# Seven block products for three pairs of k-tiles in the feed-forward layers, and for the query and output projections of attention

## The chip, the core and the metric

The kernel runs on one core of a Trainium2 chip. TensorE (PE) multiplies, VectorE (DVE) and ScalarE (ACT) do elementwise work, and SyncE (SP) issues the transfers that bring weights from memory. The metric is the time of one execution in microseconds (us), the median of several runs.

## What is computed

The reference runs one two-layer network and then another on 256 tokens of width 2048, all in float32. The parts that the change touches belong to the first network:

```python
x = x + s5_mixer(h, ...)                    # layer 0; ends in a gated projection with w_glu (GLU)
k, v = shared_kv(x, kv_norm, w_kv, k_norm)  # layer 1: rmsnorm(x, kv_norm) @ w_kv
x = x + dilated_attention(h, k, v, q_norm, w_q, w_o)   # h = rmsnorm(x, mix_norm); 3 query groups
x = x + swiglu_ffn(rmsnorm(x, ffn_norm), w_gate_up, w_down)   # after both layers
```

The second network (two mixers with projections `w_in_2` and `w_out_2`) follows; the change does not touch it.

## The kernel before

**A float32 product in three.** Every float32 operand is split in two: `hi`, its value rounded to the type fp32r of the matrix engine, and `lo`, the remainder. A product of a token tile and a weight tile is then three matmuls, hi*hi, hi*lo and lo*hi. ACT makes `whi` (a cast) and DVE makes `wlo` (the raw weight less `whi`), two tiles of 512 columns at a time (128x1024). `whi` and `wlo` have four buffers each (`WB`), and the raw ring `wraw` has two.

**Plain products.** `gemm` goes over 16 k-tiles of 128 rows and makes 512 output columns for both halves of the tokens: 16 x 2 x 3 = 96 matmuls of 512 columns.

**Paired products.** `gemm_pair` makes two blocks of 512 columns at once (a gate block and its up block; two neighbouring blocks of the down projection). The tokens' two halves and the two column blocks form a 2x2 block product, and for some of the k-tiles it is made with seven products in place of eight (Strassen's scheme in the form with four token sums S1 to S4, which `forms` has prepared, and four weight sums t1 to t4, which DVE makes each time, line 155). In what follows this is the *S phase*. It takes two pairs of k-tiles: 7 products x 2 pairs x 3 = 42 matmuls, with the weights b11, t3, t2, t4, b21, t1, b22 in this order. The other k-tiles go directly, two k-tiles to a unit of 24 matmuls (the *D phase*): 144 matmuls where there are 16 k-tiles. At the end four additions (line 230) combine the banks; for a gate-up pair ACT then makes `silu` and DVE the product `midt` (line 346, "gated"), and in the next pair's D phase the `turn` transposes `midt` on PE (8 transposes, line 269) and splits it (`act_hi` on ACT, `act_lo` on DVE). For the first chunk of each group of four `turn` also makes the token sums `mf` of the down projection (lines 115 to 124), in tiles of a pool of their own (`wt`).

**Order.** Each engine runs its instructions in the order of its own list. PE, DVE, ACT and SP have lists that a scheduler made when the kernel was built; an instruction at the head of a list that waits holds all behind it. SP issues transfers in its list's order, and each waits until the tile it overwrites has been read.

**Counts.** There are 3 pairs in the GLU stage, 10 gate-up and 6 down pairs in each feed-forward layer (`ffn` 0 and 1), and attention in four groups of heads (`hc`), each with five plain products of 16 k-tiles, then the output projection as plain products of 4 k-tiles.

Of the kernel before, what the change touches and what calls it, by code (L numbers as in the profile page):

```python
# [19 lines left out]
KT = D // 128  # L20
# [8 lines left out]
def load_unit(k, W, r0, nk, c0, cw):  # L29

    nc = k.nc
    raw = k.wraw.tile([128, 4, 512], F32, name="wraw")
    nc.sync.dma_start(
        raw[:, :nk, :cw],
        W[r0:r0 + nk * 128, c0:c0 + cw].rearrange("(k p) c -> p k c", p=128),
    )
    parts = []
    for a in range(0, nk, 2):
        n = min(2, nk - a)
        hi = k.whi.tile([128, 2, 512], F32R, name="whi")  # L40
# [14 lines left out]
def gemm(k, xT, groups, W, c0, cw, late=0):  # L55
# [18 lines left out]
    for i, g in enumerate(groups):  # L74
        with behind(k, k.lo_at), behind(k, k.sp_at):
            parts = load_unit(k, W, g[0][1], len(g), c0, cw)
# [16 lines left out]
class Strassen:  # L93
# [12 lines left out]
    def block(self):  # L106
        return self.pool.tile([128, 2, 512], F32, name="wt", bufs=3)

    def forms(self, xT, kt0, name):

        k, nc = self.k, self.k.nc
        xh, xl = (x[:, kt0:kt0 + 4, :] for x in xT)
        hi, lo = (self.pool.tile([128, 4, 2, 128], F32R, name=f"{name}_{n}") for n in ("hi", "lo"))
        x = self.block().rearrange("p q (i t) -> p (q i) t", i=2)
        nc.vector.tensor_tensor(x, xh.bitcast(F32), xl.bitcast(F32), ALU.add)
        x = x.rearrange("p (q i) t -> p q i t", i=2)
        a11, a12, a21, a22 = (x[:, :, i, t * 128:(t + 1) * 128] for t in range(2) for i in range(2))
        sm = self.block().rearrange("p a (b t) -> p (a b) t", t=128).rearrange("p (f q) t -> p f q t", q=2)
        nc.vector.tensor_tensor(sm[:, 0], a21, a22, ALU.add)
        nc.vector.tensor_tensor(sm[:, 2], a11, a21, ALU.subtract)  # L120
        nc.vector.tensor_tensor(sm[:, 1], sm[:, 0], a11, ALU.subtract)
        nc.vector.tensor_tensor(sm[:, 3], a12, sm[:, 1], ALU.subtract)
        nc.scalar.copy(hi, sm)
        nc.vector.tensor_tensor(lo, sm, hi.bitcast(F32), ALU.subtract)
        return kt0, hi, lo

    def split(self, src):

        k, nc = self.k, self.k.nc
        hi = k.whi.tile([128, 2, 512], F32R, name="whi")  # L130
        lo = k.wlo.tile([128, 2, 512], F32R, name="wlo")
# [4 lines left out]
    def gemm_pair(self, xT, forms, kts, W, row0, cols, apart=False):  # L136
# [5 lines left out]
        kt0, sh, sl = forms  # L142
        xh, xl = xT
        raw = self.pool.tile([128, 2, 2, 2, 512], F32, name="wraw4")
        for n, c0 in enumerate(cols):
            for q in range(2):
                r0 = row0 + (kt0 + 2 * q) * 128
                nc.sync.dma_start(raw[:, q, :, n, :], W[r0:r0 + 256, c0:c0 + 512].rearrange("(i p) c -> p i c", p=128))
        b11, b12, b21, b22 = (raw[:, :, i, n, :] for i in range(2) for n in range(2))
# [3 lines left out]
        def total(a, b):  # L153
            t = self.block()
            nc.vector.tensor_tensor(t, a, b, ALU.subtract)  # L155
            return t

        def product(o, form, w, start):
            wh, wl = self.split(w)
            for q in range(2):  # L160
                if form in blocks:
                    i, t = blocks[form]
                    a, b = (x[:, kt0 + 2 * q + i, t * 128:(t + 1) * 128] for x in xT)
                else:
                    a, b = (x[:, int(form[1]) - 1, q, :] for x in (sh, sl))
                nc.tensor.matmul(o, a, wh[:, q], start=start and q == 0, stop=False, skip_group_check=True)  # L166
                nc.tensor.matmul(o, a, wl[:, q], start=False, stop=False, skip_group_check=True)  # L167
                k.mm = nc.tensor.matmul(o, b, wh[:, q], start=False, stop=q == 1, skip_group_check=True).ins  # L168

        def kept(o, name):  # L170
            e = self.pool.tile([128, 512], F32, name=name)
# [17 lines left out]
        direct = [kt for kt in kts if not kt0 <= kt < kt0 + 4]  # L189
# [3 lines left out]
        def jobs():  # L193
            nonlocal called
            called += 1
            for job, rate in list(k.jobs):
                for _ in range(8 * rate * called // calls - 8 * rate * (called - 1) // calls):
# [5 lines left out]
        for g in range(last + 1):  # L203
# [7 lines left out]
            parts = [self.split(raw[:, j]) for j in range(2)]  # L211
# [111 lines left out]
def ffn(ctx, k, layer):  # L323
    nc, I = k.nc, k.I
    work = ctx.enter_context(k.tc.tile_pool(name="ffnw", bufs=2))
# [7 lines left out]
    mforms = []  # L333
    for s0 in range(0, nch, 4):
        n = min(4, nch - s0)
        mid = act_pair(k, 0)
        for c in range(s0, s0 + n):
            m = work.tile([128, 2, 512], F32, name="midt")

            def silu(t, g):  # L340
                sil = work.tile([128, 512], F32, name="sil")
# [6 lines left out]
            if c == 0:  # L348
                pg = gemm(k, xT, kgroups(), wgu, 0, 512)
                sils = [silu(t, pg[t]) for t in range(2)]  # L350
                forms = st.forms(xT, 12, "xf")
# [8 lines left out]
            def turn(m=m, c=c, s0=s0):  # L360
# [3 lines left out]
                if c == s0:  # L364
                    mforms.append(st.forms(mid, 0, "mf"))

            meanwhile(k, turn)
        for nn in range(0, 4, 2):
            pd, rest = st.gemm_pair(
                mid, mforms[-1], range(4 * n), wd, s0 * 512, (nn * 512, nn * 512 + 512), apart=True  # L370
# [543 lines left out]
def glu(ctx, k, gT):  # L914
# [21 lines left out]
    forms = st.forms(gT, 12, "xf")  # L936
# [50 lines left out]
def attention(ctx, k):  # L987
# [12 lines left out]
    xq, xkv = act_pair(k, 0), act_pair(k, 1)  # L1000
# [3 lines left out]
    split_transposed(k, xs, xkv, list(range(KT)), gkv)  # L1004
    split_transposed(k, xs, xq, list(range(KT)), gq)
# [3 lines left out]
    def project(hc):  # L1009
# [3 lines left out]
        def turned(name, pool, x, W, col, gcol):  # L1013
            kk = head_norm(k, p2, gemm(k, x, kgroups(), W, col, 512), rstd)
# [6 lines left out]
        turned("kT", p2, xkv, wkv, c0, kg)  # L1021
        vv = out["vv"] = p2.tile([128, 2, 512], F32, name="vv")
        ps = gemm(k, xkv, kgroups(), wkv, 2048 + c0, 512)
        for t in range(2):
            nc.scalar.activation(vv[:, t, :], ps[t], AF.Copy, scale=rstd[:, t:t + 1])
        for g in range(3):
            turned(f"qT{g}", p2 if g == 0 else p1, xq, wq, g * 2048 + c0, qg[:, g:g + 1])
        return out

    def heads(hc, pj):  # L1030
        yield
        kT, qT, vv = pj["kT"], [pj[f"qT{g}"] for g in range(3)], pj["vv"]
# [629 lines left out]
```

## Time and profile before

| | |
|---|---|
| median of 3 runs | 3208.32 us (3207.38 to 3209.45) |
| profiled execution: own time | 3209.36 us |
| its span | 3207.6 us |
| busy: PE, DVE, ACT | 98%, 71%, 54% of the span |
| mean granted clock of PE | 0.996 of full |

The stages follow each other along the span: the state-space mixer to about 161 us, GLU to 335, `ffn` 0 to 1045, attention to about 1640 (its transposes begin at 1043), `ffn` 1 to 2357, the second network to the end. A busy share is a mean over all of them. A matmul of 512 columns is listed with a duration of 390 ns, but matmuls are pipelined, so their cost is the distance from one start to the next.

### The profile page before, as it was taken

The numbers are of one execution on the slowest core, as the hardware profiler recorded it, in microseconds if no ns is written. First come the engines' busy times: TensorE is split into PE (matmuls) and PEld (weight loads), VectorE is DVE, ScalarE is ACT, GpSimd is POOL, SyncE is SP. The second block draws the span as 40 slices with busy tenths as digits, with TensorE's granted clock in tenths as the row PEclk, the third lists the DMA queues.
The fourth block names the chain that finished last, engine by engine and source line by source line (L and its number), as shares of the span: only waits on it lengthen the run. The fifth ranks groups of instructions, "written<-read, shape, count | busy, mean of one in ns | idle before, by whom it ended". The sixth has DMA issues, their size and how long they took to land.

```text
span 3207.6 us, 43406 instructions
## 1 busy us (share of the span) xinstructions
PE 3137.0 (98%) x16872; PEld 2671.6 (83%) x16883; DVE 2277.0 (71%) x3421; ACT 1728.8 (54%) x2335; POOL 13.8 (0%) x23
## 2 busy tenths in 40 slices
PE   4999999999999999999999999999999999999998
PEld 4788888888888888888888888888889898899887
DVE  8967777777777665756768777777858566575564
ACT  6355655455555655545455555545556455564463
POOL 1000000000000000000000000000000000000000
PEclk9999999999999999999999999999999999999999
DMA  3265655665555555454565565566555557456554
GB/s 55 85 216 171 210 182 186 209 210 194 200 197 178 171 168 177 163 189 158 168 204 186 195 201 184 182 207 210 184 162 166 184 152 221 158 165 202 155 182 170
DMA packets 343215, 573.96 MB, mean 179 GB/s; under 512 B 55073, under 2 KB 106785, under 8 KB 342177
## 3 DMA queue, kind: packets, MB, share of 16 engines
q1 hardware_dynamic: 309344, 561.91, 53.5%
q10 hardware_dynamic: 33664, 9.28, 1.4%
q8 instruction: 132, 2.16, 0.3%
q14 instruction: 75, 0.61, 0.1%
HBM read 568.51 MB, written 2.62 MB: 178 GB/s over the span
## 4 chain that ended last, share of the span: by engine, by line
PE 91%; DVE 3%; ACT 3%; DMA 2%; issue 0%; SPq 0%; ACTq 0%; another core or an unknown queue 0%; DVEq 0%
PE psg L71 14%; PE psg L69 14%; PE psg L70 14%; PE psg L220 11%; PE psg L221 11%; PE psg L222 11%; PE psg L166 4%; PE psg L167 3%; PE psg L168 3%; PE psm L269 1%; PE psg L399 1%; DMA wraw<-in_w_in 1%; DVE S L399 1%; PE psm L1044 1%; DVE sc L399 1%; ACT VW L399 1%
## 5 line engine op out<-in xcount | busy, mean ns | idle before, releaser
L43 DVE TENSOR_TENSOR wlo<-wraw,whi 128x1024 fp32r<-128x1024 f32 (+1 forms) x560 | 628.1, 1131 | 467.9 <-ACT whi L42 466.6
L42 ACT CAST whi<-wraw 128x1024 fp32r<-128x1024 f32 (+1 forms) x560 | 540.8, 978 | 640.1 <-PE psg L71 377.1
L133 DVE TENSOR_TENSOR wlo<-wraw,whi 128x1024 fp32r<-128x1024 f32 x509 | 608.4, 1222 | 279.5 <-ACT whi L132 277.1
L69 PE MATMUL psg<-whi,act_hi 128*128 128x512 f32 (+1 forms) x2144 | 802.8, 374 | 0.9 <-DVE act_lo L399 0.7
L71 PE MATMUL psg<-whi,act_lo 128*128 128x512 f32 (+1 forms) x2144 | 796.4, 372 | 4.1 <-DVE act_lo L279 4.1
L70 PE MATMUL psg<-wlo,act_hi 128*128 128x512 f32 (+1 forms) x2144 | 796.2, 371 | 0.8 <-DVE wlo L43 0.8
L132 ACT CAST whi<-wraw 128x1024 fp32r<-128x1024 f32 x509 | 522.8, 1055 | 488.7 <-DMA wraw<-in_w_gate_up 168.5
L220 PE MATMUL psg<-whi,act_hi 128*128 128x512 f32 x1616 | 630.8, 390 | 0.8 <-ACT whi L132 0.8
L221 PE MATMUL psg<-wlo,act_hi 128*128 128x512 f32 x1616 | 628.9, 389 | 0.8 <-DVE wlo L133 0.8
L222 PE MATMUL psg<-whi,act_lo 128*128 128x512 f32 x1616 | 628.8, 389 | 0.0
L71 PEld LDWEIGHTS psg<-whi,act_lo 128*128 128x128 f32 x2144 | 403.2, 188 | 59.9 <-DVE act_lo L279 5.0
L69 PEld LDWEIGHTS psg<-whi,act_hi 128*128 128x128 f32 x2144 | 403.6, 188 | 55.6 <-issue 1.3
L70 PEld LDWEIGHTS psg<-wlo,act_hi 128*128 128x128 f32 x2144 | 403.7, 188 | 53.7 <-DVE wlo L43 1.5
L220 PEld LDWEIGHTS psg<-whi,act_hi 128*128 128x128 f32 x1616 | 303.4, 188 | 63.6 <-ACT whi L132 1.2
L221 PEld LDWEIGHTS psg<-wlo,act_hi 128*128 128x128 f32 x1616 | 303.4, 188 | 63.4 <-DVE wlo L133 1.1
L222 PEld LDWEIGHTS psg<-whi,act_lo 128*128 128x128 f32 x1616 | 303.3, 188 | 63.1
L132 ACT CAST whi<-wt 128x1024 fp32r<-128x1024 f32 x140 | 147.7, 1055 | 119.7 <-PE psg L222 101.7
L133 DVE TENSOR_TENSOR wlo<-wt,whi 128x1024 fp32r<-128x1024 f32 x140 | 170.8, 1220 | 50.4 <-ACT whi L132 50.3
L155 DVE TENSOR_TENSOR wt<-wraw 128x1024 f32<-128x1024 f32 x70 | 84.3, 1220 | 8.4 <-DMA wraw<-in_w_down 6.7
L155 DVE TENSOR_TENSOR wt<-wraw,wt 128x1024 f32<-128x1024 f32 x70 | 85.5, 1221 | 1.1
L168 PE MATMUL psg<-whi,act_lo 128*128 128x512 f32 x210 | 82.0, 390 | 0.0
L167 PE MATMUL psg<-wlo,act_hi 128*128 128x512 f32 x210 | 81.9, 390 | 0.0
(359 smaller groups left out, 2931.6 us busy)
## 6 DMA issues: line engine op xcount, KB each, us to landing
wraw<-in_w_gate_up SPq DMA_DIRECT2D x320, 512.0 KB, 4.7
wraw<-in_w_down SPq DMA_DIRECT2D x176, 512.0 KB, 5.1
wraw<-in_w_in SPq DMA_DIRECT2D x96, 768.0 KB, 4.7
wraw<-in_w_q SPq DMA_DIRECT2D x48, 1024.0 KB, 5.1
wraw<-in_w_kv SPq DMA_DIRECT2D x32, 1024.0 KB, 5.5
wraw<-in_w_in SPq DMA_DIRECT2D x32, 1024.0 KB, 5.0
wraw<-in_w_out SPq DMA_DIRECT2D x32, 1024.0 KB, 5.1
wraw<-in_w_glu SPq DMA_DIRECT2D x48, 512.0 KB, 4.7
```

The source lines that it names most:

```text
L42: k.act_at = nc.scalar.copy(hi[:, :n, :cw], raw[:, a:a + n, :cw]).ins
L43: k.dve_at = nc.vector.tensor_tensor(lo[:, :n, :cw], raw[:, a:a + n, :cw], hi[:, :n, :cw].bitcast(F32), ALU.subtract).ins
L69: nc.tensor.matmul(o, a, wh, start=n == 0, stop=False)
L70: nc.tensor.matmul(o, a, wl, start=False, stop=False)
L71: k.mm = nc.tensor.matmul(o, b, wh, start=False, stop=n == total - 1).ins
L132: k.act_at = nc.scalar.copy(hi, src).ins
L133: k.dve_at = nc.vector.tensor_tensor(lo, src, hi.bitcast(F32), ALU.subtract).ins
L167: nc.tensor.matmul(o, a, wl[:, q], start=False, stop=False, skip_group_check=True)
L168: k.mm = nc.tensor.matmul(o, b, wh[:, q], start=False, stop=q == 1, skip_group_check=True).ins
L220: nc.tensor.matmul(o, a, wh[:, n], start=False, stop=False, skip_group_check=True)
L221: nc.tensor.matmul(o, a, wl[:, n], start=False, stop=False, skip_group_check=True)
L222: k.mm = nc.tensor.matmul(o, b, wh[:, n], start=False, stop=g == last and j == 1, skip_group_check=True).ins
```

## The change

The seven-product scheme now takes a list of group sizes. In GLU, in both gate-up projections and in the down projection of `ffn` 0 the sizes are (2, 1), three pairs of k-tiles: 63 matmuls in the S phase and 120 in the D phase, 183 in place of 186. The down projection of `ffn` 1 keeps two pairs, (2,). Each group has a raw tile (`sraw0` of 128x1024 per block, `sraw1` of 128x512), and every split, weight sum and form is made once per group. The weight sums t1 and t3 are computed in place over b11 and b12 (before they had tiles of their own), and t4 over t2; b21's product now stands ahead of t4's. The token sums use a tile of the ring `wraw` in place of the pool's own tiles, and in the `ffn` they are made in the turns of the first two chunks of a group in `ffn` 0, of the first in `ffn` 1.

In attention the tokens are transposed and split once (before: once for k and v, once for q). The norm weights that differ are multiplied into the weight tiles (`split_scaled`, one instruction per 512 columns on ACT and on DVE, where the plain split had one per 1024). Query groups 0 and 1 are one pair with sizes (2,), and so are the blocks of the output projection, which is now made at the end over all 16 k-tiles, two pairs, while the last heads run.

```diff
+def split_scaled(k, hi, lo, src, g):
+    k.act_at = k.nc.scalar.activation(hi, src, AF.Copy, scale=g).ins
+    k.dve_at = k.nc.vector.scalar_tensor_tensor(lo, src, g, hi.bitcast(F32), ALU.mult, ALU.subtract).ins
...
-        return self.pool.tile([128, 2, 512], F32, name="wt", bufs=3)
...
+    def fill(self, forms, xT, groups=None):
+        kt0, sizes, hi, lo = forms
+        for g in range(len(sizes)) if groups is None else groups:
+            m, q0 = sizes[g], sum(sizes[:g])
+            room = k.wraw.tile([128, 4, 512], F32, name="wraw")
...
-        raw = self.pool.tile([128, 2, 2, 2, 512], F32, name="wraw4")
...
+        for g, m in enumerate(sizes):
+            raws.append(self.pool.tile([128, m, 2, 2, 512], F32, name=f"sraw{g}"))
...
+        if gain is not None:
...
+                        nc.scalar.activation(r[:, q, i], r[:, q, i], AF.Copy, scale=gain[:, q0:q0 + 1])
...
         product(c22, "A11", b11, True)
         p1 = kept(c22, "st_p1")
-        product(c21, "S3", total(b22, b12), True)
+        t1 = less(b11, b12, b11)
+        t3 = less(b12, b22, b12)
+        t2 = less([self.pool.tile([128, m, 512], F32, name=f"wt{g}") for g, m in enumerate(sizes)], b22, t1)
+        product(c21, "S3", t3, True)
         p7 = kept(c21, "st_p7")
-        t1 = total(b12, b11)
-        t2 = total(b22, t1)
         product(c22, "S2", t2, False)
         u2 = kept(c22, "st_u2")
-        product(c21, "A22", total(b21, t2), False)
+        t4 = less(t2, b21, t2)
         product(c11, "A12", b21, True)
+        product(c21, "A22", t4, False)
...
-    work = ctx.enter_context(k.tc.tile_pool(name="ffnw", bufs=2))
+    work = ctx.enter_context(k.tc.tile_pool(name="ffnw", bufs=1))
...
+    forms = st.new_forms(KT - 6, "xf")
...
+        mforms = st.new_forms(0, "mf", (2, 1)[:2 - layer])
...
-                if c == s0:
-                    mforms.append(st.forms(mid, 0, "mf"))
+                if c - s0 < len(mforms[1]):
+                    st.fill(mforms, mid, (c - s0,))
...
-    split_transposed(k, xs, xkv, list(range(KT)), gkv)
-    split_transposed(k, xs, xq, list(range(KT)), gq)
+    split_transposed(k, xs, xT, list(range(KT)))
...
-        for g in range(3):
-            turned(f"qT{g}", p2 if g == 0 else p1, xq, wq, g * 2048 + c0, qg[:, g:g + 1])
+        pq = st.gemm_pair(xT, forms, range(KT), wq, 0, (c0, 2048 + c0), gain=gq, keep=places())
+        for g in range(2):
+            turned(f"qT{g}", p1, [pq[t][g] for t in range(2)], qg[:, g:g + 1])
+        turned("qT2", p1, gemm(k, xT, kgroups(), wq, 2 * 2048 + c0, 512, gain=gq), qg[:, 2:3])
...
+    for n in range(0, 4, 2):
+        po, rest = st.gemm_pair(
+            aT, forms, range(KT), wo, 0, (n * 512, n * 512 + 512), apart=True, keep=places()
+        )
```

**DVE around the start of a pair.** These are rows of DVE's list in `ffn` 0 where the third gate-up pair follows the second; `wraw_4716` (later `sraw_4805` and `sraw_4810`) holds the new pair's raw weights, and the lines 230 and 272, 346 and 389 are the last pair's bank additions and its gated products. Before:

```order
L133 TENSOR_TENSOR wlo<-wraw_4716,whi 128x1024
L133 TENSOR_TENSOR wlo<-wt,whi 128x1024
L230 TENSOR_TENSOR psg<-psg,st_u_4424 128x512
L230 TENSOR_TENSOR psg<-psg,st_p_4408 128x512
L155 TENSOR_TENSOR wt<-wraw_4716,wt 128x1024
L346 SCALAR_TENSOR_TENSOR midt<-psg,rstd,sil 128x512
L230 TENSOR_TENSOR psg<-psg,st_p_4394 128x512
L230 TENSOR_TENSOR psg<-psg,st_u_4458 128x512
L133 TENSOR_TENSOR wlo<-wt,whi 128x1024
L346 SCALAR_TENSOR_TENSOR midt<-psg,rstd,sil 128x512
L133 TENSOR_TENSOR wlo<-wt,whi 128x1024
L133 TENSOR_TENSOR wlo<-wraw_4716,whi 128x1024
```

After, the rows from t3's first half on; ahead of them stand `wlo` of b11 in two parts with t1's first half (line 186) between them:

```order
L186 TENSOR_TENSOR sraw_4805<-sraw_4805 128x2x512
L272 TENSOR_TENSOR psg<-psg,st_u_4523 128x512
L272 TENSOR_TENSOR psg<-psg,st_p_4504 128x512
L186 TENSOR_TENSOR sraw_4810<-sraw_4810 128x512
L389 SCALAR_TENSOR_TENSOR midt<-psg,rstd,sil 128x512
L272 TENSOR_TENSOR psg<-psg,st_p_4477 128x512
L272 TENSOR_TENSOR psg<-psg,st_u_4578 128x512
L186 TENSOR_TENSOR sraw_4810<-sraw_4810 128x512
L389 SCALAR_TENSOR_TENSOR midt<-psg,rstd,sil 128x512
L186 TENSOR_TENSOR wt_4840<-sraw_4805 128x1024
L186 TENSOR_TENSOR wt_4841<-sraw_4810 128x512
L151 TENSOR_TENSOR wlo<-sraw_4805,whi 128x1024
```

Before, the split of t3 (the second row) stands ahead of the additions; now t1, t3 and t2, each in two parts, all stand ahead of it (its first part is the last row).

**DVE where the sums for the down projection are made.** This is the D phase of the pair before that one (the second gate-up pair's turn). Before, from the first direct units' splits on (the D phase's first four k-tiles, here `x4`):

```order
L133 TENSOR_TENSOR wlo<-wraw,whi 128x1024 x4
L274 TENSOR_TENSOR act_lo<-psm,act_hi 128x512 x2
L115 TENSOR_TENSOR wt<-act_hi,act_lo 128x1024
L119 TENSOR_TENSOR wt<-wt 128x256
L120 TENSOR_TENSOR wt<-wt 128x256
L121 TENSOR_TENSOR wt<-wt 128x256
L122 TENSOR_TENSOR wt<-wt 128x256
L133 TENSOR_TENSOR wlo<-wraw,whi 128x1024 x2
L124 TENSOR_TENSOR mf_lo<-wt,mf_hi 128x1024
L133 TENSOR_TENSOR wlo<-wraw,whi 128x1024
```

After, from the last part of b22 on:

```order
L151 TENSOR_TENSOR wlo<-sraw_4453,whi 128x512
L316 TENSOR_TENSOR act_lo<-psm,act_hi 128x512 x2
L130 TENSOR_TENSOR wraw<-act_hi,act_lo 128x1024
L134 TENSOR_TENSOR wraw<-wraw 128x256
L135 TENSOR_TENSOR wraw<-wraw 128x256
L136 TENSOR_TENSOR wraw<-wraw 128x256
L137 TENSOR_TENSOR wraw<-wraw 128x256
L139 TENSOR_TENSOR mf_lo<-wraw,mf_hi 128x4x256
L151 TENSOR_TENSOR wlo<-wraw,whi 128x1024 x10
```

Four direct splits stood ahead of `act_lo` and two more ahead of `mf_lo`; now all ten stand behind `mf_lo`. ACT's list has changed in the same way: `mf_hi` now stands ahead of all ten direct `whi`.

**SP at the same place.** `wraw` with line 208 (248) are the direct units' transfers, two to a unit; `wraw_4716` and `sraw_4805` are those of the next pair's S phase. Before:

```order
L208 DMA wraw<-in_w_gate_up 128x2x512 x4
L148 DMA wraw_4716<-in_w_gate_up 128x2x512 x2
L208 DMA wraw<-in_w_gate_up 128x2x512 x4
L148 DMA wraw_4716<-in_w_gate_up 128x2x512 x2
L208 DMA wraw<-in_w_gate_up 128x2x512 x8
```

After:

```order
L170 DMA sraw_4805<-in_w_gate_up 128x2x512 x4
L248 DMA wraw<-in_w_gate_up 128x2x512 x2
L170 DMA sraw_4810<-in_w_gate_up 128x2x512
L248 DMA wraw<-in_w_gate_up 128x2x512 x2
L170 DMA sraw_4810<-in_w_gate_up 128x2x512
L248 DMA wraw<-in_w_gate_up 128x2x512 x6
```

Before, the first two units' four transfers of a D phase were ahead of the next pair's raw tile; now four of the next pair's are ahead of the first unit, in the pairs in which sums are made.

## Rows read from the trace of the kernel before

**Rows 1.** The page: span, then busy time, share and count of each engine.

```profile
span 3207.6 us, 43406 instructions
...
PE 3137.0 (98%) x16872; PEld 2671.6 (83%) x16883; DVE 2277.0 (71%) x3421; ACT 1728.8 (54%) x2335; POOL 13.8 (0%) x23
```

**Rows 2.** What PE waited for: total, times, longest.

```profile
PE psg L399 <- ACT VW L399: 39.6, 3, 36.5
PE psg L71 <- DVE act_lo L279: 4.1, 2, 2.6
PE psm L269 <- DVE x L1546: 3.9, 1, 3.9
```

**Rows 3.** A gate-up pair's S and D phase: busy time of each engine, clock, DMA.

```profile
core 0: us, PE busy (x) PEld busy (x) DVE busy (x) ACT busy (x) POOL busy (x), PEclk, DMA share, GB/s
423.24:432.80 9.56, 9.56 (x43) 7.84 (x42) 9.56 (x11) 8.99 (x12) 0.00 (x0) 1.00 0.07 14
432.80:466.00 33.20, 33.20 (x152) 27.62 (x151) 22.02 (x22) 14.17 (x16) 0.00 (x0) 1.00 0.73 250
```

**Rows 4.** DVE's timeline around the start of that pair at 423.24.

```profile
416.36 1.23 DVE L133 TENSOR_TENSOR wlo<-wraw,whi 128x1024 fp32r<-128x1024 f32 x1 [1.49 <-ACT whi L132]
419.08 1.23 DVE L133 TENSOR_TENSOR wlo<-wt,whi 128x1024 fp32r<-128x1024 f32 x1 [1.50 <-ACT whi L132]
420.23 0.69 DVE L230 TENSOR_TENSOR psg<-psg,st_u 128x512 f32<-128x512 f32 x1
...
421.43 1.22 DVE L155 TENSOR_TENSOR wt<-wraw,wt 128x1024 f32<-128x1024 f32 x1
422.56 0.74 DVE L346 SCALAR_TENSOR_TENSOR midt<-psg,rstd,sil 128x512 f32<-128x512 f32 x1
...
424.42 1.22 DVE L133 TENSOR_TENSOR wlo<-wt,whi 128x1024 fp32r<-128x1024 f32 x1
```

**Rows 5.** ACT's timeline at the same place.

```profile
415.28 1.05 ACT L132 CAST whi<-wraw 128x1024 fp32r<-128x1024 f32 x1 [1.67 <-PE psg L222]
418.00 1.05 ACT L132 CAST whi<-wt 128x1024 fp32r<-128x1024 f32 x1 [1.67 <-PE psg L222]
```

**Rows 6.** DVE's timeline where the sums for the down projection are made.

```profile
390.09 2.36 DVE L133 TENSOR_TENSOR wlo<-wraw,whi 128x1024 fp32r<-128x1024 f32 x2 [0.48 <-ACT whi L132]
392.37 1.28 DVE L274 TENSOR_TENSOR act_lo<-psm,act_hi 128x512 fp32r<-128x512 f32 x2
393.68 1.23 DVE L115 TENSOR_TENSOR wt<-act_hi,act_lo 128x1024 f32<-128x1024 f32 x1
394.94 0.43 DVE L119 TENSOR_TENSOR wt<-wt 128x256 f32<-128x256 f32 x1
395.28 0.42 DVE L120 TENSOR_TENSOR wt<-wt 128x256 f32<-128x256 f32 x1
...
399.95 1.22 DVE L124 TENSOR_TENSOR mf_lo<-wt,mf_hi 128x1024 fp32r<-128x1024 f32 x1
```

**Rows 7.** ACT's timeline there.

```profile
390.89 1.07 ACT L273 CAST act_hi<-psm 128x512 fp32r<-128x512 f32 x2
```

**Rows 8.** SP's issues at the end of that S phase.

```profile
433.13 3.35 SPq L208 DMA_DIRECT2D wraw<-in_w_gate_up  x4
```

**Rows 9.** DMA in the stretch of those issues: last columns share and GB/s.

```profile
433.10:440.00 6.90, 6.90 (x35) 5.83 (x34) 3.56 (x5) 2.61 (x5) 0.00 (x0) 1.00 1.01 351
```

**Rows 10.** PE's timeline where attention begins.

```profile
1043.76 1.91 PE L269 MATMUL psm<-ident,x 128*128 128x128 f32 x16
1045.44 0.50 PE L69 MATMUL psg<-whi,act_hi 128*128 128x512 f32 x1
```

**Rows 11.** DVE in attention by line and form: busy, mean ns, idle before.

```profile
L43 DVE TENSOR_TENSOR wlo<-wraw,whi 128x1024 fp32r<-128x1024 f32 x192 | 234.3, 1223 | 184.9 <-ACT whi L42 184.6
```

**Rows 12.** Clock (after POOL's busy time) in the state-space mixer.

```profile
105.00:110.00 5.00, 3.78 (x194) 2.95 (x197) 5.00 (x34) 1.19 (x2) 1.09 (x3) 1.00 0.15 33
110.50:120.00 9.50, 8.38 (x180) 5.61 (x171) 9.50 (x64) 2.66 (x4) 1.97 (x5) 0.50 0.36 76
```

More of the change, by code (lines that the diff above doesn't have):

```diff
@@ L104, in __init__, with new_forms @@
         self.k, self.pool = k, pool
-    def block(self):
-        return self.pool.tile([128, 2, 512], F32, name="wt", bufs=3)
-    def forms(self, xT, kt0, name):
+    def new_forms(self, kt0, name, sizes=(2, 1)):
+        return (kt0, sizes, *(self.pool.tile([128, 4, sum(sizes), 128], F32R, name=f"{name}_{n}") for n in ("hi", "lo")))
+    def fill(self, forms, xT, groups=None):
         k, nc = self.k, self.k.nc
[L112 to L125, printed above, removed]
@@ L132, in split @@
+    def split(self, src, gain=None):
+        k, nc = self.k, self.k.nc
+        m = src.shape[1]
+        hi = k.whi.tile([128, 2, 512], F32R, name="whi")[:, :m, :]
+        lo = k.wlo.tile([128, 2, 512], F32R, name="wlo")[:, :m, :]
+        if gain is not None:
+            split_scaled(k, hi, lo, src, gain)
+            return hi, lo
         k.act_at = nc.scalar.copy(hi, src).ins
@@ L150, in gemm_pair, with less @@
         c22, c21, c11, c12 = (k.psg.tile([128, 512], F32, name="psg") for _ in range(4))
         blocks = {"A11": (0, 0), "A12": (1, 0), "A22": (1, 1)}
[L153 to L156, printed above, removed]
+        def less(outs, a, b):
+            for g in range(len(sizes)):
+                nc.vector.tensor_tensor(outs[g], a[g], b[g], ALU.subtract)
+            return outs
         def product(o, form, w, start):
[L159 to L168, printed above, removed]
+            q0 = 0
+            for m, src in zip(sizes, w):
+                wh, wl = self.split(src)
+                for q in range(m):
+                    if form in blocks:
+                        i, t = blocks[form]
+                        a, b = (x[:, kt0 + 2 * (q0 + q) + i, t * 128:(t + 1) * 128] for x in xT)
+                    else:
+                        a, b = (x[:, int(form[1]) - 1, q0 + q, :] for x in (sh, sl))
+                    end = q0 + q == pairs - 1
+                    nc.tensor.matmul(o, a, wh[:, q], start=start and q0 + q == 0, stop=False, skip_group_check=True)
+                    nc.tensor.matmul(o, a, wl[:, q], start=False, stop=False, skip_group_check=True)
+                    k.mm = nc.tensor.matmul(o, b, wh[:, q], start=False, stop=end, skip_group_check=True).ins
+                q0 += m
@@ L187, in gemm_pair @@
         product(c12, "S4", b22, True)
-        direct = [kt for kt in kts if not kt0 <= kt < kt0 + 4]
+        direct = [kt for kt in kts if not kt0 <= kt < kt0 + 2 * pairs]
         calls = 1 + len(direct) // 4
@@ L210, in gemm_pair @@
                 )
-            parts = [self.split(raw[:, j]) for j in range(2)]
+            parts = [
+                self.split(raw[:, j], gain if gain is None else gain[:, pair[j]:pair[j] + 1]) for j in range(2)
+            ]
             order = [(j, t) for j in range(2) for t in range(2)]
@@ L340, in silu @@
             def silu(t, g):
-                sil = work.tile([128, 512], F32, name="sil")
+                sil = work.tile([128, 512], F32, name="sil", bufs=2 - layer)
                 nc.scalar.activation(sil, g, AF.Silu, scale=rstd[:, t:t + 1])
```

127 lines of the change are left out of this document (76 added, 51 removed).

## The prediction

> **What bounds the kernel now.** The page comes first: PE is busy for 3137.0 of 3207.6 us, DVE for 71% [rows 1]. The waits of PE show why: nearly all of what it waited for is one start-up wait of 36.5 us, and the next two entries are 4.1 and 3.9 us [rows 2]. From there on the matmuls follow each other, so time is their number times their distance. A gate-up pair's S phase has 42 matmuls in 9.56 us, 0.2276 each [rows 3]. But the same row says that DVE worked for all 9.56 us of it and ACT for 8.99, while in the D phase DVE worked for 22.0 of 33.2 us. So PE is full, and in each S phase DVE is full beside it. Such a kernel gains from fewer matmuls only where DVE can still deliver ahead of them.
>
> DVE's timeline shows how the S phase is kept fed. The pair starts at 423.24. The split of b11 ran at 416.36 and that of t3 at 419.08, both early, and at 424.42 that of t2 began, to end at 425.6; PE needs it when b11's and t3's twelve matmuls are over, at 425.98, and one matmul later (the first uses `whi` alone) [rows 4]. It was in time by about 0.6 us. ACT's casts cannot run earlier: each is released by PE giving back a `whi` buffer (415.28 and 418.00, both after a matmul of line 222) [rows 5].
>
> **What is removed.** Each third pair saves 3 matmuls: 3 pairs in GLU, 10 + 6 in `ffn` 0, 10 in `ffn` 1, so 29 x 3 = 87. In attention four query pairs save 6 each, and the two output pairs 6 each: 36. 123 x 0.2276 = 28.0 us. One of two passes of 32 x 2 transposes goes as well, of which PE's timeline gives sixteen in 1.68 us (1043.76 to 1045.44) [rows 10]: 64 - 32 = 32 transposes, 3.4 us. Together **-31.4 us**, all on the engine that bounds.
>
> **What is added in an S phase.** Prices back to back on DVE: 1024 wide 1.13 us (421.43 to 422.56), 512 wide 0.60 (420.23 to 421.43 holds two additions), a gated product about 0.66 [rows 4]. A pair with sizes (2, 1) after a gate-up pair has 7 splits and 4 weight sums of 1.13 + 0.60, four additions and two gated products: 19.0 + 2.4 + 1.3 = 22.8 us. PE's S phase grows to 63 x 0.2276 = 14.3 us. Before, it was 16.2 us of DVE for 9.56. The excess over PE grows from 6.6 to 8.5 us, and it must be worked off before the start.
>
> [...]
>
> And now the list is in the way, too. Let 0 be the start of the pair. As before, b11's first `whi` is cast at -8.0 and its `wlo` made from -6.9 to -5.7. DVE then has, in its list's order: t1's first part to -4.6, b11's second part to -4.0, t3's first to -2.8, two additions (the banks of the second token half are done at -2.7) to -1.6, t1's second part and a gated product to -0.35, two additions (the last bank ends at 0.2) to 0.85, t3's second part, a gated product, t2 in two parts: 3.9. Only then comes t3's split, 5.0. PE needs it after nine matmuls and one, at 2.3: **wait 2.8 us**. On: t3 and t2 splits to 7.4, t4 to 9.1, b21's first split to 10.3, where PE, delayed, needs it at 9.15: **wait 1.1**. The rest is in time, and the S phase ends at 18.2 in place of 14.3: 3.9 us. The same walk with the rows that stand at other places: after a down pair (no gated products, four residual additions) 1.5 + 1.1 = 2.6; after a plain product 2.5; GLU after GLU (two multiplications and two additions more) 5.1; the down pairs (2,) of `ffn` 1, 2.2 after a gate-up pair and 1.5 after a down pair.
>
> Sum: GLU 2.5 + 2 x 5.1 = 12.7; `ffn` 0: 10 x 3.9 + 5 x 2.6 + 2.5 = 54.5; `ffn` 1: 7 x 3.9 + 3 x 2.2 + 3 x 1.5 + 2 x 2.6 + 2.5 = 46.1. Together **+113 us**. Nothing lies behind it, since PE stands. Ends: DVE's work alone, 21.7 us from -5.7 on without a gap, ends at 16.0, 1.7 us behind 14.3; over 35 pairs that is 60 us. Upwards, a microsecond more in each gives 148.
>
> **The sums for the down projection.** Before, four direct splits ran ahead of `act_lo` (the last two from 390.09), and PE's D phase lived on them [rows 6]. Now `act_lo` (1.3 us for two), the sum of hi and lo (1.13), four steps of 0.34, and `mf_lo` (1.13) [rows 6] come first, with ACT's `act_hi` (1.07 for two) [rows 7] ahead and `mf_hi` (1.05, the price of a 1024 cast) in the midst. PE ends its transposes at 18.2 + 0.8 = 19.0 and needs the first direct split at 19.2. `act_lo` ends at 20.9, the sum at 22.0, the steps at 23.4, `mf_hi` at 24.5, `mf_lo` at 25.6, the split at 26.7: 7.5 us late; for one k-tile pair (128x512) the steps are half and the wait 5.9.
>
> SP makes it no better. In these pairs the next pair's four transfers stand ahead of the first unit's two. They wait until b22's first split has read the tile, at 15.5. Six transfers of 0.52 MB are 3.15 MB; at the 351 GB/s of that stretch [rows 9] 9.0 us, about 25 with the issue (0.8 us each) [rows 8]; then a cast (1.05) and a split (1.13): 27.2, **8.0 us late**. I take 8.0 for all nine such pairs, six in `ffn` 0 and three in `ffn` 1: **+72 us**. Low end 0 (as before), high end 9.
>
> **Attention.** A scaled split has twice the instructions, of 512: 1.3 for 1.13 us, about 10.6 for 9.1 us of DVE in a plain product of 96 x 0.2276 = 21.8 us. DVE waited for ACT for 184.9 us in its splits there, of 192 [rows 11], so this has cover, as have ACT's prescaled tiles. I put the boundary after each query pair at 0.6 us and the output pairs beside the last heads at 4.5: **+7 us** (0 to 15).
>
> **The sum.** -31.4 + 113 + 72 + 7 = +160.6. From the profiled execution's own 3209.4 that is 3370; that execution lies 1 us above the median of the runs, so **3369 us**.
>
> **Rivals.**
> *The whole saving shows.* If DVE gets t3's split done by 2.3 instead of 5.0, and the direct splits by 19.2, nothing waits: 3208.3 - 31.4 = 3177, faster. For it: DVE has 29% idle time over the span [rows 1]. Against: it lies in the D phases [rows 3], where no `whi` is free [rows 5]. The time falls below the old one once waits are less than 31.4 us in all, 0.7 for each of the 44 places above.
> *Only the S phases wait* (the direct splits find cover, as the sums' casts run between): 3369 - 72 = 3297.
> *Half the waits*, if PE's delay lets ACT and DVE get ahead for the next pair as well: 3208.3 - 31.4 + 96 = 3273. Against: b11's `whi` still waits for its buffer [rows 5].
> *PE's clock falls.* [...] If each of the nine 8 us waits is followed by 9.5 us at half speed, 4.75 us are lost each time, 43 in all: 3412. [...] No wait of that length stands in this trace outside the start.
>
> **Chances.** The sum as it stands 0.45; clock 0.25; only S phases 0.12; half the waits 0.10; the whole saving 0.08. The range 3285 to 3415 leaves out the last and the half-waits case. 0.2% (6.4 us) is what a measurement here can tell from no change. Slower 0.90, same 0.02, faster 0.08.
>
> **What would show it.** Right: PE's waits list `wlo` of lines 150 and 151 at the start of pairs, some 2.8 and 1.1 us each, and single waits of 6 to 9 us at a first direct unit, nine times; PE's busy time smaller by about 31 us. Wrong: DVE's split of t3 ahead of 2.3 us after a pair's start, or a D phase that begins without a wait in the pairs that make `mf`; waits in attention over 15 us would mean that the output pairs, not the pairs here, were mis-sized.

## The result, and the profile after

The changed kernel takes 3441.06 us (median of 4 runs, 3437.66 to 3443.02) against 3207.85 us; the ratio is 1.0726, 95% interval 1.0707 to 1.0745. It is slower, as forecast, but by 233 us where 161 were forecast, and 26 us above the upper end of the range.

The page of the changed kernel, the lines that answer to [rows 1]:

```profile
span 3440.7 us, 44043 instructions
...
PE 3206.3 (93%) x16728; PEld 2674.8 (78%) x16728; DVE 2481.8 (72%) x3844; ACT 1862.3 (54%) x2620; POOL 13.2 (0%) x23
```

PE has fewer matmuls and yet is busy for 69 us longer (the prediction looked for 31 less), since a matmul that is slow is listed as busy (in the D phases below, 30.56 us at a mean clock of 0.89 and 27.30 at 1.00): the mean granted clock of this run was 0.973 (before 0.996). With the rest of the time at 0.50, that is by estimate 2 x 0.027 x 3440.7 = 186 us at the low level, where the kernel before has 2 x 0.004 x 3207.6 = 26 us.

What PE waited for in the changed kernel, as in [rows 2] (us in all, times, longest):

```profile
PE psg L262 <- ACT whi L150: 77.8, 10, 9.4
PE psg L200 <- ACT whi L150: 52.1, 54, 2.9
PE psg L442 <- ACT VW L442: 39.2, 3, 36.2
PE psg L201 <- DVE wlo L151: 18.4, 19, 2.9
PE psg L80 <- ACT whi L53: 8.4, 3, 4.2
```

The third row is the start-up wait that was there before. The first is the first direct unit where the sums are made; the second and fourth are the S phases; the last is new and was not forecast.

A gate-up pair of the changed kernel, S phase with its eight transposes and D phase, as in [rows 3] (length, busy time of PE, PEld, DVE, ACT and POOL, clock, DMA share, GB/s):

```profile
510.38:530.60 20.22, 17.71 (x73) 13.58 (x71) 18.52 (x22) 14.13 (x20) 0.00 (x0) 0.92 0.09 25
530.60:557.90 27.30, 27.30 (x123) 22.60 (x122) 17.57 (x20) 11.34 (x14) 0.00 (x0) 1.00 0.81 290
```

Without a wait the S phase would be 14.3 + 0.8 = 15.1 us long. The D phase is full, 120 x 0.2276 = 27.3. DVE's timeline around the start of that pair (510.35), as in [rows 4]:

```profile
503.48 1.22 DVE L151 TENSOR_TENSOR wlo<-sraw,whi 128x1024 fp32r<-128x1024 f32 x1 [1.49 <-ACT whi L150]
...
506.48 1.22 DVE L186 TENSOR_TENSOR sraw<-sraw 128x1024 f32<-128x1024 f32 x1
507.62 0.69 DVE L272 TENSOR_TENSOR psg<-psg,st_u 128x512 f32<-128x512 f32 x1
...
512.53 1.81 DVE L186 TENSOR_TENSOR wt<-sraw 128x1024 f32<-128x1024 f32 x2
514.26 1.82 DVE L151 TENSOR_TENSOR wlo<-sraw,whi 128x1024 fp32r<-128x1024 f32 x2
...
519.48 1.82 DVE L151 TENSOR_TENSOR wlo<-sraw,whi 128x1024 fp32r<-128x1024 f32 x2
521.53 1.83 DVE L151 TENSOR_TENSOR wlo<-wt,whi 128x1024 fp32r<-128x1024 f32 x2 [0.24 <-ACT whi L150]
524.32 3.66 DVE L151 TENSOR_TENSOR wlo<-sraw,whi 128x1024 fp32r<-128x1024 f32 x4 [0.96 <-ACT whi L150]
```

The walk of the prediction is here row by row: b11's split at -6.9, t3's first part at -3.9, additions from -2.7, t2 at 2.2, t3's split at 3.9 in place of -4.2 [rows 4], b21's at 9.1. PE's timeline of the same pair shows what followed on the wait:

```profile
514.93 0.51 PE L200 MATMUL psg<-whi,xf_hi 128*128 128x512 f32 x1 [2.14 <-ACT whi L150]
515.54 0.50 PE L201 MATMUL psg<-wlo,xf_hi 128*128 128x512 f32 x1
515.88 0.57 PE L202 MATMUL psg<-whi,xf_lo 128*128 128x512 f32 x1
516.24 0.63 PE L200 MATMUL psg<-whi,xf_hi 128*128 128x512 f32 x1
516.67 0.63 PE L201 MATMUL psg<-wlo,xf_hi 128*128 128x512 f32 x1
```

ACT had cast t3's `whi` by 512.8 and cast t2's from 513.83, right after DVE's sum t2. So the row of 514.93, which waits for a `whi`, is taken to be t2's first matmul, which PE's list has between t3's first and second; that would explain why most of these waits are listed under the cast and not, as the prediction expected, under `wlo`. The row after it needs t3's `wlo`, 515.54 where 512.6 was planned. Then the distance between matmuls goes from 0.23 to 0.43 us: the clock fell after a wait listed with 2.14 us, to 0.50 from 515.94 to 519.35.

A pair in which sums are made, S and D phase, and the stretches around its long wait:

```profile
696.40:724.40 28.00, 16.60 (x72) 12.41 (x71) 21.74 (x29) 14.37 (x21) 0.00 (x0) 0.93 0.40 134
724.40:755.00 30.60, 30.56 (x120) 24.56 (x121) 18.81 (x19) 12.51 (x13) 0.00 (x0) 0.89 0.44 152
```
```profile
721.00:724.00 3.00, 0.00 (x0) 0.00 (x0) 1.23 (x1) 1.03 (x2) 0.00 (x0) 0.50 1.09 355
724.00:731.00 7.00, 6.56 (x15) 4.70 (x16) 4.53 (x4) 3.29 (x4) 0.00 (x0) 0.50 0.94 328
```

The S row's 28.0 us hold the wait, and in the D phase PE is full for 30.6 us where 27.3 would do, at half speed until 731. The timelines of PE, DVE, ACT and SP at that wait, one fence each:

```profile
724.40 1.22 PE L262 MATMUL psg<-whi,act_hi 128*128 128x512 f32 x2 [8.50 <-ACT whi L150]
```
```profile
721.36 1.23 DVE L139 TENSOR_TENSOR mf_lo<-wraw,mf_hi 128x1024 fp32r<-128x1024 f32 x1 [1.11 <-ACT mf_hi L138]
724.38 2.36 DVE L151 TENSOR_TENSOR wlo<-wraw,whi 128x1024 fp32r<-128x1024 f32 x2 [1.79 <-ACT whi L150]
```
```profile
720.29 1.04 ACT L138 CAST mf_hi<-wraw 128x1024 fp32r<-128x1024 f32 x1 [3.71 <-DVE wraw L137]
723.30 1.99 ACT L150 CAST whi<-wraw 128x1024 fp32r<-128x1024 f32 x2 [1.97 <-DMA wraw<-in_w_gate_up]
```
```profile
712.58 1.91 SPq L170 DMA_DIRECT2D sraw<-in_w_gate_up  x4
714.59 1.04 SPq L248 DMA_DIRECT2D wraw<-in_w_gate_up  x2
```

SP issued the next pair's four transfers at 712.58 and the first unit's two behind them; ACT was done with `mf_hi` at 721.3 and then stood 1.97 us for that transfer. So both chains of the prediction are there, and the transfers end 2 us later than the sums. PE lost 8.50 us, forecast 8.0.

### The profile page after: what moved, and what is told of

Its sections match the earlier page's. It is cut to its first block, busy times and chain, and to the rows that moved or that the text cites. A ratio compares the mean times of both kernels' runs of the same rounds, so it can differ in the third digit from the quotient of the medians.

```text
span 3440.7 us, 44043 instructions
## 1 busy us (share of the span) xinstructions
PE 3206.3 (93%) x16728; PEld 2674.8 (78%) x16728; DVE 2481.8 (72%) x3844; ACT 1862.3 (54%) x2620; POOL 13.2 (0%) x23
## 4 chain that ended last, share of the span: by engine, by line
PE 65%; DVE 16%; DMA 8%; ACT 6%; issue 4%; SPq 1%; ACTq 0%; DVEq 0%
PE psg L81 10%; PE psg L82 10%; PE psg L80 9%; DVE wlo L151 7%; PE psg L262 7%; PE psg L263 7%; PE psg L264 7%; DMA wraw<-in_w_gate_up 5%; ACT whi L150 3%; PE psg L201 3%; PE psg L202 3%; PE psg L200 3%; PE psm L442 2%; DVE sraw L186 2%; DMA wraw<-in_w_down 1%
## 5 line engine op out<-in xcount | busy, mean ns | idle before, releaser
L262 PE MATMUL psg<-whi,act_hi 128*128 128x512 f32 x1672 | 660.9, 396 | 79.1 <-ACT whi L150 77.8
L151 DVE TENSOR_TENSOR wlo<-wraw,whi 128x1024 fp32r<-128x1024 f32 x370 | 439.5, 1222 | 341.3 <-ACT whi L150 336.0
L54 DVE TENSOR_TENSOR wlo<-wraw,whi 128x768 fp32r<-128x768 f32 (+1 forms) x368 | 393.7, 1083 | 297.1 <-ACT whi L53 296.5
L150 ACT CAST whi<-wraw 128x1024 fp32r<-128x1024 f32 x370 | 375.2, 1050 | 426.1 <-DMA wraw<-in_w_gate_up 214.6
L53 ACT CAST whi<-wraw 128x768 fp32r<-128x768 f32 (+1 forms) x368 | 339.4, 939 | 393.7 <-PE psg L82 171.6
L150 ACT CAST whi<-sraw 128x1024 fp32r<-128x1024 f32 x350 | 299.1, 873 | 252.5 <-PE psg L264 99.2
L151 DVE TENSOR_TENSOR wlo<-sraw,whi 128x1024 fp32r<-128x1024 f32 x350 | 339.1, 998 | 49.1 <-ACT whi L150 48.7
L32 DVE SCALAR_TENSOR_TENSOR wlo<-wraw,gain,whi 128x512 fp32r<-128x512 f32 (+1 forms) x240 | 196.0, 852 | 90.9 <-ACT whi L31 90.3
L31 ACT ACTIVATE whi<-wraw,gain 128x512 fp32r<-128x512 f32 (+1 forms) x240 | 181.1, 802 | 113.9 <-DMA wraw<-in_w_q 43.1
L200 PE MATMUL psg<-whi,xf_hi 128*128 128x512 f32 x324 | 136.3, 421 | 33.8 <-ACT whi L150 33.7
L201 PE MATMUL psg<-wlo,xf_hi 128*128 128x512 f32 x324 | 138.7, 428 | 12.2 <-DVE wlo L151 11.5
```

Source lines behind the costliest of these rows:

```text
L54: k.dve_at = nc.vector.tensor_tensor(lo[:, :n, :cw], raw[:, a:a + n, :cw], hi[:, :n, :cw].bitcast(F32), ALU.subtract).ins
L150: k.act_at = nc.scalar.copy(hi, src).ins
L151: k.dve_at = nc.vector.tensor_tensor(lo, src, hi.bitcast(F32), ALU.subtract).ins
L200: nc.tensor.matmul(o, a, wh[:, q], start=start and q0 + q == 0, stop=False, skip_group_check=True)
L262: nc.tensor.matmul(o, a, wh[:, n], start=False, stop=False, skip_group_check=True)
```

## The experiments

Each kernel is the changed one with the edit shown, unless it says otherwise; each time is a median beside the kernel before on the same chip.

**Sums one call later.**

```diff
+            def turn_steps(turn=turn, c=c):
+                with k.tc.issue_after(k.mm):
+                    turn()
+                yield
+                if c - s0 < len(mforms[1]):
+                    yield
+                    with k.tc.issue_after(k.mm):
+                        st.fill(mforms, mid, (c - s0,))
+                    yield
+            start(k, turn_steps())
```

> The changed kernel, but the sums for the down projection are made one job call later, after the first two direct units (DVE: three direct splits, act_lo, a fourth, then the sums). Theory A (the nine long waits at the first direct unit come from the sums standing ahead of the direct splits and of the transfers, and each is followed by a stretch at the lower clock): the waits of 78 us on line 262 go, and so do some eight stretches of 10.2 us at half clock, 5.1 us each: 3441 - 78 - 41 = about 3322 us. Theory B (the low clock only stretches time that would be waited through anyway): 3441 - 78 = about 3363. Theory C (the wait is the transfers', held behind the next pair's raw tile wherever the sums are made): no change, 3441.

3364.7 us, ratio 1.0491 (1.0475 to 1.0507): 76 us less. Its waits of PE:

```profile
PE psg L200 <- ACT whi L150: 61.6, 63, 3.1
...
PE psg L201 <- DVE wlo L151: 20.3, 18, 3.0
...
PE psg L262 <- ACT whi L150: 6.7, 5, 2.8
```

The long waits went from 77.8 to 6.7 us, so where the sums stand in the lists made them; theory C is out. (DVE's list and SP's changed together, so the run does not part their shares; the timelines above do.) The mean clock rose from 0.973 to 0.985, some 85 us less of low clock. The time is theory B's number, but not for B's reason. From first matmul to first matmul in the two traces, the long waits take 80 us less; the nine D phases behind them take 12 less, having lost nearly all of their low clock (in the changed kernel's trace eight stretches of 10.2 us and one of 6.8) but gained some waits; and the S phases of three pairs take 16 more. 80 + 12 - 16 is the 76.

**t2 after t3's split.**

```diff
-        t2 = less([self.pool.tile([128, m, 512], F32, name=f"wt{g}") for g, m in enumerate(sizes)], b22, t1)
         product(c21, "S3", t3, True)
         p7 = kept(c21, "st_p7")
+        t2 = less([self.pool.tile([128, m, 512], F32, name=f"wt{g}") for g, m in enumerate(sizes)], b22, t1)
```

> The changed kernel, but the weight sum t2 is made after t3's split instead of ahead of it. DVE's work in the S phase is the same, so the waits there keep their sum, but the first, of 2.2 to 3 us, becomes two of 1.0 to 1.5. Theory A (the clock falls after single waits of 2 us and more): the 15 short low stretches of 3.4 us in S phases go, 1.7 us each, so 3441 - 25 = about 3416, and the waits listed are shorter singly but not in sum. Theory B (low clock costs nothing): 3441, the same within 0.2%. Theory D (t3's late split is the whole S-phase cost): the first wait falls by 1.7 us in 26 pairs, 3441 - 45 = about 3396, without a later wait taking its place.

3441.9 us, ratio 1.0731 (1.0715 to 1.0747): no change.

```profile
PE psg L201 <- DVE wlo L151: 47.3, 51, 2.1
...
PE psg L200 <- ACT whi L150: 30.2, 50, 1.0
```

The waits became shorter singly and 7 us more in sum (77.5 for 70.5), and the clock's mean rose to 0.980. Theory D is out: moving one split ahead only moves the wait to the next. The low clock in S phases that went was replaced by waits, so this run does not tell what it cost; the next one does.

**Matmuls in the waits.** Their results are not read; the rest is computed as before.

```diff
+        def filler(n):
+            with k.tc.issue_after(k.mm):
+                pt = k.psm.tile([128, 512], F32, name="psm")
+                for i in range(n):
+                    k.mm = nc.tensor.matmul(pt, xh[:, 0, 0:128], xh[:, 0:2, :], start=True, stop=True).ins
...
+                    if form == "S3" and q0 + q == 0 and pairs == 3:
+                        filler(9)
...
+        if k.filled:
+            filler(26)
```

> The changed kernel with added matmuls, whose results nothing reads, in the places where TensorE waits: 9 of 512 columns (2.05 us) after t3's first matmul in each pair of sizes (2, 1), 26 (5.9 us) ahead of the first direct unit where sums are made. They are shorter than the waits they stand in, so the data come no sooner and no later. Theory A (the low clock after the waits costs about 80 us by itself): the granted clock stays near 0.996 and the time falls to about 3441 - 70 = 3371. Theory B (the low clock costs nothing that the waits do not already cost): 3441, and if the added matmuls stand in the way, a little more.

3424.8 us, ratio 1.0679 (1.0658 to 1.0700): 16 us less, by the two ratios' intervals some 6 to 24. The pair that answers to the one at 510.38, with the nine added matmuls in PE's timeline:

```profile
508.48:527.60 19.12, 18.39 (x82) 14.10 (x80) 18.43 (x22) 13.93 (x20) 0.00 (x0) 1.00 0.09 24
```
```profile
510.77 2.21 PE L211 MATMUL psm<-act_hi 128*128 128x512 f32 x9
```

The clock stayed at 1.00, and the S phase took 19.12 in place of 20.22 us: 15.1 + 4.0, which is the walk's 3.9. So in such a pair the low clock cost 1.1 us. Over the kernel the mean rose to 0.991 (62 of 186 us left), and the gain is neither A's 70 nor B's nothing. By the traces, the S phases of three pairs take 13 us less and the D phases 13 less; the waits at the direct units, with the added matmuls in them, take 3 more; and 10 of what was won is hidden by the second network, which neither edit touches (855 us here, 845 in the changed kernel's trace).

**Two pairs everywhere.** `(2,)` for `(2, 1)` in GLU and both feed-forward layers.

> The changed kernel with sizes (2,) everywhere, so 42 matmuls in each S phase and sums for the down projection in one turn of four; in-place sums, their order, the ring tile for the sums, and attention stay as changed. Theory A (the order of the sums and of the splits makes the waits, the third pair only enlarges them): waits of some 2.0 us after a gate-up pair and 1.6 after a down pair remain, as do six long waits of 8 us with 5 us of low clock each: 29 x 3 more matmuls (+20), 3 long waits fewer (-39), S phases -66: about 3356. Theory E (the third pair itself makes the loss): the waits go, about 3215.

3352.9 us, ratio 1.0452 (1.0434 to 1.0469). Theory A's number, 3356. The third pair, with three of the nine long waits and the second ring tile that go with it, makes 88 of the 233 us; the larger part is there without it. The plain products ahead of `ffn` 0's first pair take 44.5 us again, as before the change.

**Attention alone, and without the output pairs.** GLU and the feed-forward layers are those of the kernel before; the second kernel also keeps the old order of the output projection.

```diff
+    def output(hc):
+        for n in range(4):
+            po = gemm(k, aT, kgroups(4, hc * 512, hc * 4), wo, n * 512, 512)
...
+    for hc in range(HCH):
+        start(k, heads(hc, project(hc)))
+        if 0 < hc < HCH - 2:
+            output(hc - 1)
```

> The change in attention alone; GLU and both feed-forward layers as in the kernel before. The changed kernel's trace has attention 5.2 us longer than before (594.5 to 599.7 us from its first transposes to the next layer's). If that is attention's own cost, 3208 + 5 = about 3213 us. If it was lengthened by what came before it (late banks and buffers after the down pairs), the saving forecast shows: 3208 - 5 = about 3203, with waits of under 8 us.

> As the last, but the output projection as before (plain products of four k-tiles each, spread over the stage); the one transposition, the norm weights in W and the query pairs stay. If the output pairs beside the last heads make the loss: -4 x 1.4 (query pairs) - 3.4 (transposes) + 2 (boundaries) = -7, about 3201 us, faster than before. If the scaled splits or the boundaries after the query pairs make it: 3208 to 3213.

3217.2 us, ratio 1.0031 (1.0019 to 1.0042), and 3202.3 us, ratio 0.9985 (0.9977 to 0.9994). The change in attention loses 11 us; the second kernel is 4 us below the kernel before (2 to 7 by the interval). So the output projection made in pairs at the end, beside the last heads, costs about 15 us; the run does not part the pairs from their new place. Attention from its first transposes to the next layer's, in the kernel before, with the whole change in attention, and without the output pairs:

```profile
1043.80:1638.30 594.50, 593.69 (x2833) 496.23 (x2832) 387.28 (x731) 315.23 (x431) 0.00 (x0) 1.00 0.54 174
```
```profile
1043.80:1644.40 600.60, 591.49 (x2767) 487.64 (x2766) 451.93 (x854) 382.27 (x561) 0.00 (x0) 0.99 0.52 169
```
```profile
1041.50:1634.10 592.60, 588.69 (x2777) 489.08 (x2776) 445.36 (x854) 371.26 (x546) 0.00 (x0) 1.00 0.52 172
```

The first of the two new ones has 9 us in which PE is idle; the other has 4. The last row is only 1.9 us shorter than the first; the second network, from its first transposes to the end, differs by 5 us between these two traces and takes from 845 to 856 us in the traces of this study, though the change does not touch it. So of the 4 us some 2 are seen where the change was made.

**t3 in a tile of its own, two pairs.** It is the kernel with `(2,)` and t3's sum and product ahead of t1 and t2 in the three stages (not in attention).

```diff
+            t3 = less([self.pool.tile([128, m, 512], F32, name=f"wu{g}") for g, m in enumerate(sizes)], b22, b12)
         product(c21, "S3", t3, True)
         p7 = kept(c21, "st_p7")
+        if own:
+            t1 = less(b11, b12, b11)
+            t2 = less([self.pool.tile([128, m, 512], F32, name=f"wt{g}") for g, m in enumerate(sizes)], b22, t1)
```

> Sizes (2,) everywhere as in the run with two pairs (3353), but t3 has a tile of its own and its product stands ahead of t1 and t2 again, in GLU and layer 0's feed-forward and, as the space allows, layer 1's. Theory A (in-place sums put t3's split behind t1, t2 and the additions): the S phases run without waits as before, 17 x 2.3 + 7 x 1.6 + 4 less, so 3353 - 54 = about 3299, with the six long waits for the sums left. Theory F (cutting nothing but DVE's total work matters): the same, 3353.

3328.4 us, ratio 1.0378 (1.0364 to 1.0392): 24 us less than with two pairs, not 54. t1 is still made in place, behind b11's split, and b21's product still stands ahead of t4's; what is left in an S phase was not taken apart further.

> The last kernel with the sums for the down projection made one job call later. Theory A: the six long waits and the low clock after them go too, 6 x 11 = 66 less: about 3233, and less where the sums now hide wholly; what is left above 3208 is attention's part. Theory C (the long waits are the transfers'): 3299.

3268.0 us, ratio 1.0188 (1.0173 to 1.0204): 60 less, the six long waits. A gate-up pair's S phase is 11.9 us here, with the clock at 1.00, where the kernel before has 9.56 and eight transposes, 10.4:

```profile
430.30:442.20 11.90, 11.18 (x50) 8.56 (x51) 10.86 (x12) 9.77 (x13) 0.00 (x0) 1.00 0.09 27
```

This kernel is still 60 us above the kernel before, and attention's 11 explain only part of that. Its largest waits of PE in S phases, none of which the kernel before has:

```profile
PE psg L201 <- DVE wlo L151: 9.8, 19, 1.3
PE psg L200 <- ACT sil L392: 7.0, 17, 0.4
```

The rest of the change (t1 in place, b21 ahead of t4, pools with one buffer in place of two, the ring tile for the sums) was not tested part by part, so some 50 us stay open.

**t3 in a tile of its own, three pairs** (in GLU and `ffn` 0), and the same with the sums one call later.

> The changed kernel with sizes (2, 1), but in GLU and layer 0's feed-forward t3 has tiles of its own and its sum and product stand ahead of t1 and t2 (layer 1 has no space for them). Theory A (half of the S-phase wait is the list's order, half is DVE's work for three pairs in 63 matmuls): the walk with this order gives waits of 0.7 at t2 and 1.4 at b21, so 2.1 in place of 3.9 us after a gate-up pair and no 3.4 us clock stretch; 10 pairs x 2.8 + 7 others x 1.3 = 37 less: about 3404. Theory G (the third pair as such cannot be fed): under 10 us less, above 3431. Theory H (order is everything): the S phases of layer 0 and GLU run without waits, 65 less: 3376.

> The last kernel with the sums for the down projection one job call later, as in the run that gave 3365 by that alone. If the two faults are independent: 3365 + (what the last run gives) - 3441, about 3328 by theory A. If the long waits hide the others (a late D phase gives DVE time to get ahead of the next pair), less than that is gained: above 3340.

3418.3 us, ratio 1.0665 (1.0640 to 1.0690), and 3343.2 us, ratio 1.0419 (1.0404 to 1.0435). 23 less, between theories A and G. The S phase after a gate-up pair, 17.60 us for 20.22, has 2.5 us of waits where the walk gave 2.1:

```profile
508.80:526.40 17.60, 15.88 (x72) 12.18 (x70) 16.52 (x20) 13.88 (x20) 0.00 (x0) 1.00 0.09 27
```

Both edits together save what they save one by one (76 + 23, measured 98), so the S phases' waits and the long waits are independent faults.

## Why the prediction was right in its signs and wrong in its size

The waits that the sum named were all in the trace, at their places. What was mis-sized or left out:

- **S phase after a gate-up pair: 3.9 us, measured 5.1** in the pair shown (20.22 - 15.1). Of the 17 such pairs, 13 have a stretch of low clock in the S phase and lie 5.0 to 5.8 us above their 14.3; the four others lie 4.0 to 4.1 above. So the walk itself was right, and the missing 1 us is the low clock, which the prediction put into a rival and there only behind the 8 us waits. PE's row at the wait and the S phase without its transposes, for a pair with the low clock and one without:

```profile
456.54 0.50 PE L200 MATMUL psg<-whi,xf_hi 128*128 128x512 f32 x1 [2.14 <-ACT whi L150]
759.58 0.50 PE L200 MATMUL psg<-whi,xf_hi 128*128 128x512 f32 x1 [2.14 <-ACT whi L150]
```
```profile
451.97:471.30 19.33, 16.82 (x65) 12.75 (x64) 16.41 (x20) 11.29 (x16) 0.00 (x0) 0.91 0.06 13
755.00:773.37 18.37, 15.58 (x64) 11.64 (x63) 16.33 (x20) 11.16 (x16) 0.00 (x0) 1.00 0.07 15
```

- **The other S phases.** After a down pair 2.6 was forecast: two down pairs of `ffn` 0 took 17.2 us, 2.8 over 14.3, and `ffn` 1's gate-up pairs 17.1; but `ffn` 0's two gate-up pairs took 19.4 and 19.7, 5.1 and 5.4 over, with a low stretch in each. `ffn` 1's down pairs took 12.34 and 11.3 us, 1.9 and 1.7 over (2.2 and 1.5 forecast). GLU after GLU was 4.3 over, where 5.1 was forecast. In all, the S phases are 130 us over, 17 more than the 113 of the sum, about as much as 15 low stretches at 1.1.
- **Sums for the down projection: 8.0 us forecast, 8.5 in the pair shown**; all nine come to 80 where the sum has 72. But the D phase behind each took 2 to 3.4 us more than its 27.3, PE being full at the low clock (in the pair shown 30.6 us, at 0.50 until 731): 25 us in all, for which the sum had no term.
- **The plain product in which the next sums (`xf`) are made.** It had a term only for the S phase behind it (2.5). `ffn` 0's first two plain products took 49.8 us in place of 44.5, and with the transposes `ffn` 1's took 58.7 for 49.3; GLU's 4 more: 19 us. The prediction did not follow `fill` to this place. ACT and SP there:

```profile
370.23 1.99 ACT L53 CAST whi<-wraw 128x1024 fp32r<-128x1024 f32 x2 [0.88 <-DMA wraw<-in_w_gate_up]
```
```profile
365.06 8.99 SPq L39 DMA_DIRECT2D wraw<-in_w_gate_up  x3
```

  The sums for (2, 1) take both tiles of the ring, so SP could issue no weights until 365.06, when those in the first tile were done, and PE waited 2.7 us on the cast and ran at 0.50 from 372.6 to 376.0. In the run with sizes (2,) everywhere the same stretch is 44.5 us: one tile stays free.
- **Attention: -4.6 forecast (-11.6 saved, +7 waits); the part measured alone is +11.** The output pairs beside the last heads were given 4.5 us, from no row, with 2.7 of saving against it; net, they and their new place cost some 15. In the changed kernel's trace the stage itself is 5.2 us longer than before, 10 more than forecast.

These misses in the changed kernel's trace, 17 + 8 + 25 + 19 + 10, come to 79 where 72 are missing. The 19 are partly attention's (with the change in attention alone `ffn` 1 was 6 us longer as well), and the second network, from its first transposes on, took 7 us less than in the trace of before, and the time ahead of GLU 2 less, which no part of the change explains.

**The step that failed** is the choice of the likeliest case: the sum has nothing for the clock, whose fall was a rival with a chance of 0.25, behind the nine long waits alone. It rested on a wrong reading of the trace of before, as if the low clock of [rows 12] were its only stretch and nothing had followed on the wait of 3.9 us [rows 2]. That trace has two more at waits of PE, the 3.9 us one and one of 2.65 us, each with the clock at 0.50 as PE goes on:

```profile
2360.21 0.69 PE L71 MATMUL psg<-whi,act_lo 128*128 128x384 f32 x1 [2.65 <-DVE act_lo L279]
2780.49 2.82 PE L269 MATMUL psm<-ident,x 128*128 128x128 f32 x12 [3.94 <-DVE x L1546]
```
```profile
2359.80:2363.20 3.40, 2.99 (x10) 2.89 (x11) 3.40 (x8) 2.84 (x8) 0.00 (x0) 0.50 0.13 9
2779.70:2786.50 6.80, 6.01 (x24) 5.92 (x25) 6.10 (x13) 5.81 (x17) 0.00 (x0) 0.50 0.65 158
```

So the forecast waits of 2.8 us already asked for a term. What the runs showed in its place is a cost of about 17 us in fifteen S phases (an estimate, 15 x 1.1) and of 25 us in nine D phases. That the two together come to the rival's 43 is luck: it had 4.75 us behind each of nine waits (half of the 9.50 us in [rows 12]), where 2 to 3.4 were measured, and nothing in S phases. By the low clock alone (3369 + 42) the result would still have been inside the range. Two further terms put it outside: the plain product with `xf`, which had none and took 19 us, and attention's output pairs, given 4.5 us.

What the low clock costs is also smaller than its 186 us suggest. Half of them, 93 us, would by estimate be lost if PE had worked throughout; keeping PE busy through the waits took two thirds of the low clock away (62 of 186 us left) and gave back 16 us, about 26 in the S and D phases themselves. In the two pairs above, PE's next listed wait, before 463.18 and 764.81, is 0.27 us in the one with the low clock and 0.47 in the other: some of the time that the slow PE lost it would have waited through.

The rival that the whole saving shows needed t3's split by 2.3 us after the pair's start and direct splits by 19.2; they came at 5.0 and about 29. What the change was good for is seen without the new waits: one transposition and the query pairs, some 2 to 4 us.

## What to carry to other kernels

Where one engine is full and another is full beside it in one phase, count the second engine's work in that phase before taking work off the first: seven products for three pairs take 3 of 186 matmuls away and add 6.6 us of VectorE's work (22.8 for 16.2, the prediction's estimate) to a phase in which it had no time to spare (9.56 us busy of 9.56 [rows 3]). A tile taken from a ring for scratch space also took a transfer's turn here (49.8 us for 44.5); ask what SP can no longer issue while it is held. And a sum made in place is a new order: everything that reads the old value must come first, also on the engine whose list decides. Before calling a fall of the clock unlikely, look up every low stretch of the trace, and what ended just ahead of it.

## What the runs showed of the hardware that was not expected

The granted clock fell to 0.50 after waits of 2.09 to 2.90 us in fifteen S phases; the first pair shown above is one, at 516 to 519 us, and the kernel before has it after 2.65 us. But the same wait was not always followed by a fall: of the two pairs shown side by side, both with 2.14 us before t2's first matmul, one fell (0.91 over its S phase) and one did not (1.00), and the difference in length is 1.0 us. In these pairs, in which PE waits again later (0.27 and 0.47 us), the fall cost less than the slower matmuls alone would: a stretch of 3.4 us at half speed is 1.7 us of work, but 1.0 us parts these two pairs, and 1.1 us parts the pair with the added matmuls from the one without.
